# A planner that orders a hybrid decoder step: DVE and POOL take their shared port in turn, and three kinds of matmul get other prices

## The chip, the core and the metric

The kernel runs on one core of a Trainium2 chip. The metric is the device time of one execution in microseconds (us). Engines are named as in the profile: PE is the matrix engine (PEld its weight loads), DVE the vector engine, ACT the scalar engine, POOL the GpSimd engine, SP the queue that issues nearly all DMAs.

## The reference, cut to what matters

One layer on 1024 prompt tokens and 32 sample tokens of width 1024, in float32:

```python
h   = rms_norm(x, norm_mix_w) * (1 + scale_m) + shift_m     # scale, shift, gate from c @ w_ada
p   = h @ w_in
y_a = rwkv7_mixer(...)        # 6 heads of 64, delta rule
y_b = gated_deltanet_mixer(...)   # 6 heads of 64, chunks of 64 tokens
y_c = hgrn2_mixer(...)        # 4 heads of 64, chunks of 64 tokens
x   = x + gate_m * (concat(y_a, y_b, y_c) @ w_out)
h2  = rms_norm(x, norm_ffn_w) * (1 + scale_f) + shift_f
gate, up = split(h2 @ w_ffn_in)
x   = x + gate_f * ((silu(gate) * up) @ w_ffn_out)
y   = rms_norm(x, final_norm_w)
```

The states of the mixers are outputs too. A mixer goes through the chunks one after the other: in a B mixer (`gated_delta_chunked`) each chunk needs the state S that the chunk before it left.

## The kernel before, in words

The kernel is not written in the order in which it runs. Its functions only record operations on a `Plan` object (class `Plan`). Then `nc.order()` (line 2053) decides the order of the whole program, and `emit` (line 619) issues the operations in that order; each engine runs its own in order. About 12,300 matmuls, 4,000 DVE, 2,400 ACT, 1,100 POOL operations and 990 DMAs of SP are recorded. All are issued from line 626 in `emit`, so every row of the profile has the line L626, and tiles tell the rows apart.

`cost` (line 399) gives each operation a price, `hold`, the time for which it keeps its engine, and `LAT` and `SEEN` the time until others see its result. `order` (line 467) walks through a time of its own. At each step it takes the engine that is free first, moves to it the operations whose inputs are there by that time, and issues the one with the lowest key (line 479: the place in the recording, plus a priority). So prices never change what is computed; they change which operations count as ready when an engine comes free, and thereby the order. Two further rules matter on PE. The dense products (float32r, 256 and more moving columns, below written as dense matmuls) of the projections carry a priority that puts them behind everything else, so they fill the time in which the mixers' small matmuls are not ready. And a rule that counts the columns issued lately puts dense matmuls first where the array's clock would fall.

The work, in the order of the recording:

1. Norm and projections (`dense`, line 1501). A float32 product is done as three float32r passes over halves: `wh` times the high part, `wh` times the low part, `wl` times the high part (`dmm`, line 1493). `wh` is rounded by ACT, `wl` is the difference, taken by POOL or DVE (`wtile`, line 1461).
2. Eight mixers (three A, three B, two C) in three segments each; the projections of one run beside the mixer before. `seg_b` (line 1175) has the chunk loop of mixer B: matmul with S, `zs` on DVE, matmul, `us` on ACT, `sd` on POOL, matmul, new S on DVE. Pairs of 64x64 matmuls on the two halves of the rows are issued together (`mm2`, line 721). A triangular inverse per segment is a chain of small DVE operations on the tiles `itq` and `ix`.
3. Output projection, then the feed-forward part, in two halves g = 0 and g = 1 of 528 columns. For each of 22 blocks of 128 rows, `ffn_up` (line 1729) makes seven block products of 12 dense matmuls with 264 columns; their weight sums (tiles `wr`, `int`, `s`, `tq`) and splits (`wl`) go to POOL or DVE by the string `ENGW` (line 70). After each two blocks `down` (line 2018) adds 16 products to the residual with DVE (`gated_half`, line 1789: tiles `kp`); in g = 1 the sample columns need two more DVE operations each (`gated_seq`, line 1798: `ga`, then `kp<-kp,ga`).
4. The final norm.

All four engines' placements (which engine does what) are fixed in the recording.

Of the kernel before, what the change touches and what calls it, by code (L numbers as in the profile page):

```python
# [21 lines left out]
P = 128  # L22
TP = 1024
NQ = 8
TQ = 4
TS = NQ * TQ
T = TP + TS
# [142 lines left out]
ENG = {"tensor": mybir.EngineType.PE, "vector": mybir.EngineType.DVE, "scalar": mybir.EngineType.Activation,  # L170
       "gpsimd": mybir.EngineType.Pool, "sync": mybir.EngineType.SP}
LAT = {"tensor": 158, "vector": 92, "scalar": 110, "gpsimd": 45, "sync": 900}       # result visible after the engine
SEEN = {"tensor": 100, "vector": 36, "scalar": 38, "gpsimd": 64, "sync": 60}        # wait for another engine
# [6 lines left out]
class Tile:  # L180
    def __init__(self, plan, tag, dt):
        self.plan, self.tag, self.dt = plan, tag, dt
        self.slot = self.fresh = self.ap = None
        self.first = None          # first op
        self.left = 0
        self.ops = []
        self.end = 0
        self.writes, self.reads = [], []


class View:
    """a view of a tile whose place is not decided yet; kept as the view of the first place and the way to it"""
# [37 lines left out]
class Op:  # L230
    __slots__ = ("i", "eng", "fn", "args", "kw", "pre", "succ", "npre", "hold", "lat", "ready", "prio", "cols", "wait", "dense", "new", "tiles",
                 "label", "end", "start", "after", "x", "next", "load")
# [10 lines left out]
class Plan:  # L243
    """stands for nc and the tile pools while a program is written down"""
# [15 lines left out]
    # ---- tiles  # L260
    def tile(self, pool, shape, dt, tag, bufs=1, like=None):
        """like: a view of the same shape; such a tag takes both float32 and float32r"""
# [3 lines left out]
        t = Tile(self, tag, dt)  # L266
# [5 lines left out]
    def give(self, tag, to, cut):  # L272
        """once the last tile of tag is done with, the parts that cut makes of its places hold tiles of the tag to"""
        for ap in self.phys[tag]:
            for part in cut(ap):
                self.gifts.setdefault(tag, []).append((to, len(self.phys[to])))
                self.phys[to].append(part)
# [10 lines left out]
    # ---- what a view covers  # L288
    def cover(self, v):
# [6 lines left out]
        else:  # L296
            ps = ap.ap[0][0]
# [4 lines left out]
        if m is None:  # L302
            m = 1
            for s, n in dims:
# [4 lines left out]
                while k < n:  # L309
                    c = min(k, n - k)  # L310
                    # add c more copies
# [6 lines left out]
    # ---- writing down  # L318
# [29 lines left out]
    def glue(self, ops):  # L348
        """to be issued one right after the other, once all of them can be"""
# [14 lines left out]
    def dep(self, o, p, kind):  # L364
        # kind 2: result needed, 1: only the order matters
# [32 lines left out]
    # ---- prices  # L398
    def cost(self, o):
# [7 lines left out]
        e = o.eng  # L407
        if e == "tensor":
# [11 lines left out]
            # hold: how long the next one has to wait; load: how long after the one before the weights are there  # L420
# [5 lines left out]
            elif r:  # L426
                o.hold = max(M, n) / 2.4 + 3 if n >= 256 else max(M / 1.2, n / .6)
            elif K <= 32 and M <= 32:
                o.hold = 56 if p0 == 32 else 27
            elif K <= 64 and M <= 64:  # L430
                o.hold = 27 if p0 >= 64 else 2 * max(M, n) / 1.2 + 3
# [34 lines left out]
    # ---- the order  # L466
    def order(self):
# [12 lines left out]
        # queue of the tiles of each tag  # L480
# [16 lines left out]
        bw = [0.0]  # L497
        warm = {}
# [15 lines left out]
        def grant(tag):  # L514
            q, f = queue[tag], free[tag]
            while f and head[tag] < len(q):
                # earliest free place
# [15 lines left out]
        while len(seq) < n:  # L533
# [39 lines left out]
            if e == "tensor":  # L573
                if last:
                    tm = max(tm, last.start + o.load * (2 if last.x > last.hold else 1))
                last = o
            o.start = tm
# [65 lines left out]
class Step:  # L643
# [7 lines left out]
    # tiles of one tag are given out in program order, so every stream of work has its own  # L651
# [73 lines left out]
    def tokens(self, arrs, c, nch):  # L725
        """chunk c of each array [(h, d), tokens] -> psum [64 tokens, array, h, d]; two chunks are turned at once"""
# [8 lines left out]
    def headsum(self, x, n, which="bones", alloc=None):  # L735
        """sum or mean over the channels of a head, on each of its channels; the ones are exact in float32r"""
# [8 lines left out]
    def sigmoid(self, out, x, nbias=0.0, sign=1.0):  # L745
        """sigmoid(sign * x - nbias) from the one table set that has exp and ln"""
# [12 lines left out]
    def table(self, name, behind=None, before=None):  # L759
        """load a set of functions, behind one activation and before another"""  # L760
# [7 lines left out]
    # tt[(h,s), c, t] holds N^T, N = -(strictly lower part); on return it holds ((I - N)^-1)^T  # L768
    def invert(self, tt, nc_):
# [11 lines left out]
        # one 32x32 block and every fourth column of it per partition:  # L781
        # nt[p, j, i] = N[i, j]; x[p, m, i] = X[i, 4m + cg], X = (I - N)^-1
# [26 lines left out]
        # (T21)^T = (N21 T1)^T T2^T  # L809
# [24 lines left out]
    def raw_a(self):  # L834
        """three segments of [last column of the one before | columns]; the last one ends in 8 x (prev, 4 samples)"""
# [19 lines left out]
    def shift_mix(self, out, r, mu, si):  # L855
        """out = p + mu * (prev - p)"""
# [26 lines left out]
    def mixer_a(self, g, rps, st0, outs):  # L883
        """rps: raw segments of r, k, v; st0 dram [128 (h,dk), 8, 64]; outs: prompt state, sample states, y"""
# [9 lines left out]
    def seg_a(self, g, si, rps, Ss, st0, outs):  # L894
# [70 lines left out]
        for c in range(nch):  # L965
# [13 lines left out]
            # one bank per chunk: z, u, new state, output; a group starts on the operand that comes last  # L979
# [51 lines left out]
    def sample_state(self, xs, st0):  # L1031
        """rows of x^T S0_q of each sequence's own tokens, 32 per x and head"""
# [46 lines left out]
    def raw_b(self, cst):  # L1079
        """three segments of [3 columns before | columns]; the last one ends in 8 x (3 before, 4 samples)"""  # L1080
# [28 lines left out]
    def evac_gates(self, gd):  # L1109
        """rows 0-5 beta_pre, rows 32-37 a_pre of one segment (rounded weights; the rest of the weights 64 rows on)  # L1110
        -> beta, g, exp(g_last - g) of the tokens [(h, token), which, pair, chunk], and beta, g as rows in dram"""
# [7 lines left out]
        def f(si, ps):  # L1119
# [12 lines left out]
            # g = -exp(A_log) * softplus(a + dt_bias)  # L1132
# [11 lines left out]
            # exp(g_last - g)  # L1144
# [30 lines left out]
    def seg_b(self, g, si, rps, z, Ss, st0, outs):  # L1175
# [76 lines left out]
        # the rows of (I - N)^-1 times beta: what it multiplies is v - k S  # L1252
# [58 lines left out]
    def evac_plain(self, z, pad=None):  # L1311
        """the projection as it is; the padding of the last segment"""
# [15 lines left out]
    def lower_bound(self):  # L1328
        nc = self.nc
        # softmax over the depth axis (one layer), then cumsum minus the first layer's share  # L1330
# [16 lines left out]
    def seg_c(self, j, si, q, pf, v, z, Ss, st0, outs):  # L1347
# [39 lines left out]
        def fill(out, mask, data, last, lm):  # L1387
            """the places of A that the mask names; last: of the chunk of the sequences"""
# [4 lines left out]
        # a token with itself and with the one in front of it: products summed over the channels  # L1393
# [67 lines left out]
    def wtile(self, w, eng=None):  # L1461
        """w: dram [128, n, 128] -> for each of the n tiles hi (rounded to the float32r grid), lo = w - hi (exact)"""
# [15 lines left out]
    def wtile_narrow(self, w):  # L1478
        """w: 64 columns, twice: hi of the first half of the columns, lo of the second"""
# [13 lines left out]
    def dmm(self, o, terms, first=True, last=True):  # L1493
        """o = sum of w^T x over terms ((w hi, w lo), (x hi, x lo))"""
# [6 lines left out]
    def dense(self, w, xs, chunks, evac, banks=None, wt=None, warm=0):  # L1501
        """banks: one for each chunk; the products then go through the rows of w first"""
        nc = self.nc
        with self.nc.priority(-LOW):
            wt = wt or self.wtile(w)
            term = lambda k, a, b: (wt[k], (xs[k][0][:, a:b], xs[k][1][:, a:b]))
            if banks:
                pss = [bk() for bk in banks]
                # the array's clock rises with work: products that nothing reads, while the first
                # operands are still on their way  # L1510
# [664 lines left out]
```

## Time and profile before

| what | value |
|---|---|
| three runs | 1862.27, 1865.06, 1881.21 us, median 1865.06 us |
| profiled execution, first to last instruction (span) | 1864.7 us |
| PE busy | 1715.9 us, 92% of the span |
| DVE busy | 1557.1 us, 84% |
| ACT busy, POOL busy | 952.0 us (51%), 958.8 us (51%) |
| TensorE clock granted, mean over the span | 0.953 of full speed |

The profile gives the span of the profiled execution and no other time of it; the span lies 0.4 us below the median of the three runs. Busy time of PE holds modelled ends of pipelined matmuls. A DVE operation that waits for something within its execution counts as busy there.

### The profile page before, as it was taken

Reading aid. Unit: us, or ns where it says so; the run is one execution under the profiler, and the core shown is the slowest. Engines: PE = TensorE matmul, PEld = TensorE weight load, DVE = VectorE, ACT = ScalarE, POOL = GpSimd, SP = SyncE. Lnnn points to the kernel's source line nnn. Section 1 sums busy time; section 2 is a strip of 40 time slices with the busy share of each in tenths; the row PEclk is TensorE's granted clock in tenths of the full one; section 3 lists DMA queues with packets and bytes.
Section 4 is the critical chain, followed back from the end, with each engine's and each line's share of the span. In section 5 each row is a group of like instructions: output and inputs, shape, how many; then the busy total and the mean of one; then the engine's idle time right before and its main releaser. Section 6 shows DMA issues by size and latency. Waiting matters only on the chain.

```text
span 1864.7 us, 42417 instructions
## 1 busy us (share of the span) xinstructions
PE 1715.9 (92%) x15462; PEld 1483.8 (80%) x15462; DVE 1557.1 (84%) x3981; ACT 952.0 (51%) x2383; POOL 958.8 (51%) x1089
## 2 busy tenths in 40 slices
PE   4999999899899789899999999999998889999996
PEld 2777766667677677677679999999998789999995
DVE  6776688879879877887776999889999999899998
ACT  4543454655556455656874655444444543443444
POOL 5542333433335544636523866656567555555555
PEclk8989999889999898999989999999999799999998
DMA  7424123123224222211353222323232132232231
GB/s 264 124 64 116 39 62 109 49 68 113 59 77 127 55 63 55 57 34 39 102 155 115 66 93 95 108 91 109 91 103 69 62 115 79 91 108 85 87 108 65
DMA packets 151242, 166.56 MB, mean 89 GB/s; under 512 B 65941, under 2 KB 91161, under 8 KB 151033
## 3 DMA queue, kind: packets, MB, share of 16 engines
q1 hardware_dynamic: 150456, 163.27, 28.8%
q8 instruction: 121, 1.98, 0.5%
q14 instruction: 89, 0.72, 0.1%
q10 hardware_dynamic: 576, 0.59, 0.1%
HBM read 149.23 MB, written 14.57 MB: 88 GB/s over the span
## 4 chain that ended last, share of the span: by engine, by line
PE 52%; DVE 28%; issue 6%; POOL 5%; ACT 4%; SPq 2%; DMA 2%; DVEq 0%; POOLq 0%; ACTq 0%
PE psd L626 16%; PE psc L626 13%; PE psm L626 11%; PE psg L626 11%; DVE sl L626 6%; DVE itq L626 5%; DVE ix L626 5%; DVE kp L626 3%; SPq L626 2%; POOL wl L626 2%; DVE s L626 2%; ACT sl L626 2%; DVE wl L626 2%; DVE wr L626 2%; DVE act L626 1%
## 5 line engine op out<-in xcount | busy, mean ns | idle before, releaser
L626 PE MATMUL psd<-act,wh 128*128 128x384 f32 (+3 forms) x2144 | 552.8, 334 | 13.2 <-ACT act L626 7.4
L626 PEld LDWEIGHTS psd<-act,wh 128*128 128x128 f32 x2144 | 373.9, 195 | 40.8 <-ACT act L626 8.9
L626 POOL TENSOR_TENSOR wl<-wr,wh 128x512 fp32r<-128x512 f32 (+1 forms) x216 | 300.7, 1396 | 192.1 <-ACT wh L626 177.3
L626 PE MATMUL psd<-act,wl 128*128 128x384 f32 (+3 forms) x1048 | 348.9, 333 | 5.3 <-DVE wl L626 3.8
L626 ACT ACTIVATE sl<-sl 128x384 f32<-128x384 f32 (+5 forms) x400 | 188.1, 484 | 129.2 <-DVE sl L626 101.4
L626 ACT CAST wh<-wr 128x512 fp32r<-128x512 f32 (+1 forms) x280 | 170.7, 615 | 109.0 <-PE psd L626 27.8
L626 PEld LDWEIGHTS psd<-act,wl 128*128 128x128 f32 x1048 | 203.7, 194 | 21.2 <-DVE wl L626 6.2
L626 DVE TENSOR_TENSOR itq<-int,ix 96x66 f32<-96x66 f32 (+26 forms) x558 | 170.7, 306 | 27.1 <-DMA int<-mb 15.9
L626 DVE TENSOR_TENSOR ix<-ix,itq 96x66 f32<-96x66 f32 (+26 forms) x558 | 164.7, 295 | 9.6
L626 PE MATMUL psg<-act,wh 128*128 128x264 f32 (+2 forms) x784 | 154.2, 290 | 5.3 <-DVE act L626 4.0
L626 PE MATMUL psc<-act,wh 128*128 128x264 f32 (+2 forms) x776 | 152.4, 289 | 0.8 <-DVE act L626 0.6
L626 PE MATMUL psm<-act,wh 128*128 128x264 f32 (+1 forms) x760 | 147.8, 288 | 2.7 <-ACT act L626 1.3
L626 POOL TENSOR_TENSOR sl<-sl,sl 128x384 fp32r<-128x384 f32 (+5 forms) x84 | 85.5, 1019 | 101.2 <-ACT sl L626 39.2
L626 PEld LDWEIGHTS psg<-act,wh 128*128 128x128 f32 x784 | 124.6, 191 | 7.5 <-DVE act L626 4.9
L626 ACT CAST raw<-sl 128x264 fp32r<-128x264 f32 x88 | 36.3, 413 | 173.7 <-DVE sl L626 92.5
L626 PEld LDWEIGHTS psc<-act,wh 128*128 128x128 f32 x776 | 123.1, 190 | 2.4 <-DVE act L626 1.1
L626 PEld LDWEIGHTS psm<-act,wh 128*128 128x128 f32 x760 | 119.5, 190 | 4.5 <-ACT act L626 1.5
L626 POOL TENSOR_TENSOR wl<-int,wh 128x512 fp32r<-128x512 f32 (+1 forms) x63 | 87.9, 1398 | 61.1 <-ACT wh L626 61.0
L626 PE MATMUL psc<-act,wl 128*128 128x264 f32 (+2 forms) x388 | 113.4, 292 | 5.4 <-DVE wl L626 3.7
L626 PE MATMUL psg<-act,wl 128*128 128x264 f32 (+2 forms) x392 | 114.0, 291 | 2.6 <-DVE wl L626 2.1
L626 PE MATMUL psm<-act,wl 128*128 128x264 f32 (+1 forms) x380 | 110.2, 290 | 4.4 <-DVE wl L626 3.0
L626 ACT COPY ts<-psg 64x128 f32<-64x128 f32 (+1 forms) x272 | 75.9, 279 | 69.1 <-PE psc L626 46.1
(324 smaller groups left out, 4481.3 us busy)
## 6 DMA issues: line engine op xcount, KB each, us to landing
wr<-in_w_fi_dram SPq DMA_DIRECT2D x87, 256.0 KB
wr<-in_w_ada_dram SPq DMA_DIRECT2D x80, 256.0 KB
wr<-in_w_in_dram SPq DMA_DIRECT2D x62, 256.0 KB
wr<-in_w_fo_dram SPq DMA_DIRECT2D x51, 256.0 KB
int<-in_w_fi_dram SPq DMA_DIRECT2D x46, 256.0 KB
kp<-in_xT_dram SPq DMA_DIRECT2D x32, 192.0 KB
tq<-in_w_fi_dram SPq DMA_DIRECT2D x23, 256.0 KB
s<-in_w_fi_dram SPq DMA_DIRECT2D x20, 256.0 KB
```

Source lines behind the costliest of these rows:

```text
L626: getattr(getattr(nc, o.eng), o.fn)(*[real(a) for a in o.args], **{k: real(a) for k, a in o.kw.items()})
```

## The change

Four edits; everything else that differs in the file is comments, and line numbers (line 626 of before is line 634 of after).

1. Each operation gets a mark `port`. It is set for a POOL operation with an SBUF input of more than one element per partition, for a DVE operation with two such inputs, and for a DVE `tensor_scalar` or `tensor_copy` with one.
2. In `order`, a marked operation starts no earlier than the end of the marked operation before it, on whichever of the two engines that was. The operation has been chosen by then, so its engine waits with it.
3. A float32r matmul with n >= 256 columns is priced n/2.4 + 12 instead of n/2.4 + 3 ns (264 columns: 122 instead of 113; 384 columns: 172 instead of 163).
4. A 64x64 float32 matmul is priced 58 ns in either half of the rows, instead of 110 in the upper and 27 in the lower half.

```diff
@@ cost
         e = o.eng
+        sb = [a for a in list(o.args[1:]) + list(o.kw.values()) if isinstance(a, View) and self.space[a.t.tag] == "sb" and size(a) > 1]
+
+        o.port = e == "gpsimd" and len(sb) > 0 or e == "vector" and (
+            len(sb) > 1 or len(sb) == 1 and o.fn in ("tensor_scalar", "tensor_copy"))
         if e == "tensor":
...
             elif r:
-                o.hold = max(M, n) / 2.4 + 3 if n >= 256 else max(M / 1.2, n / .6)
+                o.hold = max(M, n) / 2.4 + 12 if n >= 256 else max(M / 1.2, n / .6)
             elif K <= 32 and M <= 32:
                 o.hold = 56 if p0 == 32 else 27
             elif K <= 64 and M <= 64:
-                o.hold = 27 if p0 >= 64 else 2 * max(M, n) / 1.2 + 3
+                o.hold = 2 * max(M, n) / 2.4 + 5
@@ order
         bw = [0.0]
+        port = 0
...
+            if o.port:
+                tm = max(tm, port)
+                port = tm + o.hold
             o.start = tm
```

The order of all engines changes from the first products on. Three places follow, each before and after.

PE in the last B mixer, at the chunk loop of `seg_b` (`zs`, `sd`, `us` and `S` are its steps, `psd<-act` are dense matmuls of a projection). Before:

```order
L626 MATMUL psd_151<-act_123,wh_100 128x384
L626 MATMUL psc_117<-zs_185,kp_68 64x64 x2
L626 MATMUL psd_151<-act_124,wh_100 128x384
L626 MATMUL psd_151<-act_123,wl_105 128x384
L626 MATMUL psd_151<-act_125,wh_100 128x384
L626 MATMUL psd_151<-act_126,wh_100 128x384
L626 MATMUL psd_151<-act_125,wl_105 128x384
L626 MATMUL psd_151<-act_127,wh_102 128x384
L626 MATMUL psc_117<-sd_190,ts_184 64x64 x2
L626 MATMUL psd_151<-act_128,wh_102 128x384
```

The same place after:

```order
L634 MATMUL psc_117<-S_176,kp_86 64x64 x2
L634 MATMUL psg_153<-msk_63,kp_80 128x128
L634 MATMUL psg_153<-msk_63,kp_78 128x128
L634 MATMUL psc_117<-zs_185,kp_68 64x64 x2
L634 MATMUL psc_117<-sd_189,ts_184 64x64 x2
L634 MATMUL psc_117<-kp_84,us_187 64x64 x2
L634 MATMUL psc_117<-kp_69,S_176 64x64 x2
L634 MATMUL psc_118<-S_177,kp_86 64x64 x2
```

The dense matmuls that stood between the steps of the chunk are gone from here; they now stand earlier, in longer rows of their own.

PE in the second half of the feed-forward part, at the first use of a `wl` that DVE makes (`wl_105`, used by `psd_151`). Before:

```order
L626 MATMUL psm_112<-act_121,wl_104 128x264
L626 MATMUL psd_151<-act_123,wh_100 128x264
L626 MATMUL psd_151<-act_124,wh_100 128x264
L626 MATMUL psd_151<-act_123,wl_105 128x264
```

The same place after:

```order
L634 MATMUL psd_151<-act_123,wh_100 128x264
L634 MATMUL psd_151<-act_124,wh_100 128x264
L634 MATMUL psc_118<-act_127,wh_102 128x264
L634 MATMUL psc_118<-act_128,wh_102 128x264
L634 MATMUL psc_118<-act_127,wl_107 128x264
L634 MATMUL psc_118<-act_127,wh_102 128x264
L634 MATMUL psc_118<-act_128,wh_102 128x264
L634 MATMUL psc_118<-act_127,wl_107 128x264
L634 MATMUL psc_118<-act_127,wh_102 128x264
L634 MATMUL psd_151<-act_123,wl_105 128x264
```

Seven matmuls of another product have moved in between the two that need only `wh` and the one that needs `wl`.

DVE at the same block, from the end of the residual additions (`kp`, `ga`) to that `wl_105`. Before:

```order
L626 SCALAR_TENSOR_TENSOR kp_87<-psd_150,mod_89,kp_87 128x232
L626 TENSOR_TENSOR ga_213<-psd_150,mod_89 128x32
L626 TENSOR_TENSOR wl_105<-int_113,wh_100 128x512
L626 TENSOR_TENSOR kp_87<-kp_87,ga_213 128x32
L626 TENSOR_TENSOR sl_1039_38269<-sl_1038_38244,psc_117 128x264
L626 TENSOR_TENSOR wl_107<-wr_99,wh_102 128x512
```

The same place after:

```order
L634 SCALAR_TENSOR_TENSOR kp_87<-psd_150,mod_89,kp_87 128x232
L634 TENSOR_TENSOR ga_213<-psd_150,mod_89 128x32
L634 TENSOR_TENSOR wr_97<-tq_202,int_113 128x512
L634 TENSOR_TENSOR kp_87<-kp_87,ga_213 128x32
L634 TENSOR_TENSOR sl_1039_38253<-sl_1038_38228,psc_117 128x264
L634 TENSOR_TENSOR wl_107<-wr_97,wh_102 128x512
L634 TENSOR_TENSOR wr_96<-wr_97,wr_96 128x512
L634 TENSOR_TENSOR wl_105<-tq_202,wh_100 128x512
```

The weight sums `wr` of this block, which DVE did between the residual additions before, now come behind them, and `wl_107` comes ahead of `wl_105`.

## Rows read from the trace of the kernel before

**Rows 1.** The profile's first part: busy us (share of span), instructions.

```profile
PE 1715.9 (92%) x15462; PEld 1483.8 (80%) x15462; DVE 1557.1 (84%) x3981; ACT 952.0 (51%) x2383; POOL 958.8 (51%) x1089
```

**Rows 2.** Busy us by stretch: length, PE, PEld, DVE, ACT, POOL, PEclk, DMA share, GB/s.

```profile
100.00:910.00 810.00, 744.04 (x7775) 567.56 (x7775) 638.97 (x2016) 441.07 (x1260) 345.77 (x548) 0.94 0.25 69
...
1050.00:1435.00 385.00, 379.91 (x3068) 375.02 (x3067) 351.39 (x691) 182.83 (x376) 240.60 (x182) 1.00 0.30 95
1435.00:1500.00 65.00, 49.34 (x269) 42.33 (x270) 62.18 (x110) 37.27 (x84) 43.26 (x40) 0.74 0.21 66
1500.00:1840.00 340.00, 325.03 (x2588) 318.65 (x2588) 313.34 (x742) 142.17 (x281) 189.31 (x137) 0.99 0.28 90
```

**Rows 3.** Chain that ended last, shares by line: 100 to 910, then 1500 to 1840.

```profile
by line: PE psd L626 18.7%; PE psc L626 11.5%; DVE itq L626 10.8%; DVE ix L626 10.7%; PE psm L626 7.1%; DVE sl L626 7.1%; PE psg L626 6.4%; SPq L626 5.1%; issue 3.7%; ACT sl L626 3.2%; DVE kp L626 2.8%; DMA int<-mb 1.8%; DVE s L626 1.4%; DV
...
by line: PE psg L626 14.9%; PE psm L626 14.9%; PE psc L626 14.3%; issue 13.5%; PE psd L626 13.1%; POOL wl L626 7.8%; DVE wl L626 4.2%; DVE wr L626 4.1%; DVE kp L626 3.3%; DVE sl L626 2.8%; DVE int L626 1.4%; POOL wr L626 1.4%; DVE tq L626 1
```

**Rows 4.** PE's longest waits, 100 to 910: us in total, times, longest us.

```profile
PE psm L626 <- DVE sl L626: 12.9, 10, 3.1
PE psc L626 <- DVE S L626: 9.2, 9, 2.0
```

**Rows 5.** Timeline of PE in mixer A: start us, us, what [idle before].

```profile
193.04 0.33 PE L626 MATMUL psd<-act,wl 128*128 128x384 f32 x1
193.21 0.34 PE L626 MATMUL psd<-act,wh 128*128 128x384 f32 x1
193.48 0.56 PE L626 MATMUL psg<-kp,kp 64*64 64x64 f32 x12
193.98 0.44 PE L626 MATMUL psd<-act,wh 128*128 128x384 f32 x1
194.25 0.34 PE L626 MATMUL psd<-act,wl 128*128 128x384 f32 x1
```

**Rows 6.** Timeline of four engines, one chunk of mixer B.

```profile
693.11 0.33 PE L626 MATMUL psc<-zs,kp 64*64 64x64 f32 x4
...
693.53 0.21 ACT L626 COPY us<-psc 128x64 f32<-128x64 f32 x1 [0.19 <-issue]
...
693.82 0.29 POOL L626 TENSOR_TENSOR sd<-us,tok 128x64 f32<-128x64 f32 x1 [3.72 <-ACT us L626]
...
694.62 0.33 PE L626 MATMUL psc<-sd,ts 64*64 64x64 f32 x4
...
695.09 0.28 DVE L626 SCALAR_TENSOR_TENSOR S<-S,dl,psc 128x64 f32<-128x64 f32 x1 [0.69 <-PE psc L626]
...
697.80 0.33 PE L626 MATMUL psc<-zs,kp 64*64 64x64 f32 x4 [0.56 <-DVE zs L626]
```

**Rows 7.** Timeline of PE in the second half of the feed-forward part.

```profile
1654.94 0.40 PE L626 MATMUL psd<-act,wh 128*128 128x264 f32 x2
1656.00 0.39 PE L626 MATMUL psd<-act,wl 128*128 128x264 f32 x1 [0.65 <-DVE wl L626]
1656.22 0.40 PE L626 MATMUL psd<-act,wh 128*128 128x264 f32 x2
1656.46 0.29 PE L626 MATMUL psd<-act,wl 128*128 128x264 f32 x1
```

**Rows 8.** Timeline of DVE in the same stretch.

```profile
1653.07 1.28 DVE L626 TENSOR_TENSOR kp<-kp,ga 128x32 f32<-128x32 f32 x1
...
1655.87 0.18 DVE L626 TENSOR_TENSOR kp<-kp,ga 128x32 f32<-128x32 f32 x1
...
1663.89 0.42 DVE L626 TENSOR_TENSOR sl<-sl,psm 128x264 f32<-128x264 f32 x1
```

**Rows 9.** Timeline of POOL in the same stretch.

```profile
1652.83 1.47 POOL L626 TENSOR_TENSOR wl<-tq,wh 128x512 fp32r<-128x512 f32 x1 [0.57 <-ACT wh L626]
...
1663.73 1.40 POOL L626 TENSOR_TENSOR wl<-wr,wh 128x512 fp32r<-128x512 f32 x1 [1.33 <-ACT wh L626]
```

**Rows 10.** PE's longest wait from 1500 to 1840.

```profile
PE psc L626 <- DVE wl L626: 3.3, 5, 0.7
```

More of the change, by code (lines that the diff above doesn't have):

```diff
@@ L231 @@
     __slots__ = ("i", "eng", "fn", "args", "kw", "pre", "succ", "npre", "hold", "lat", "ready", "prio", "cols", "wait", "dense", "new", "tiles",
-                 "label", "end", "start", "after", "x", "next", "load")
+                 "label", "end", "start", "after", "x", "next", "load", "port")
 class Engine:
```

## The prediction

> **What bounds the kernel now.** I read the profile's first part, then the busy times by stretch, the chain of waits for two of the stretches, PE's waits, and last the timeline at single places. The reader is to see first that PE is busy for 1715.9 of 1864.7 us and DVE for 1557.1 [rows 1]: two engines near their limit, with 149 us of idle PE to be had. The table by stretch [rows 2] says where. In the first half of the feed-forward part (1050 to 1435) PE idles 385.0 - 379.9 = 5.1 us: it is the bound. In the second half (1500 to 1840) it idles 340.0 - 325.0 = 15.0 us, beside a DVE that is busy 313.3 of 340. At the change of halves (1435 to 1500) PE idles 15.7 us at a granted clock of 0.74, with DVE busy 62.2 of 65. In the mixers (100 to 910) it idles 810.0 - 744.0 = 66.0 us at a clock of 0.94. What is left of the 149 lies in the first 100 us, around the output projection and in the last 25 us.
>
> The chain [rows 3] tells the two kinds of stretch apart. In the mixers PE's four banks have 18.7 + 11.5 + 7.1 + 6.4 = 43.7% of it, DVE's inverse alone (`itq`, `ix`) 21.5%: the path passes to and fro between engines. From 1500 on PE's banks have 57.2%, and POOL's and DVE's weight tiles most of the rest.
>
> **The port is real.** The DVE operation `kp<-kp,ga` with 32 elements took 1.28 us from 1653.07 to 1654.35, and 0.18 us at 1655.87 [rows 8]. POOL's `wl` ran from 1652.83 to 1654.30 [rows 9]: DVE waited to its end. At 1663.89 `sl<-sl,psm`, with one input in PSUM, took 0.42 us though POOL's `wl` ran from 1663.73 to 1665.13 [rows 8, 9]. So edits 1 and 2 mark the right operations, and the old planner placed matmuls behind DVE results that come up to a microsecond later than it thought.
>
> **Edits 3 and 4.** Two dense matmuls of 264 columns start 1656.46 - 1656.22 = 0.24 us apart [rows 7], 0.12 each as now priced (before: 0.113); with 384 columns 193.21 - 193.04 = 0.17 [rows 5], as now priced. Six 64x64 matmuls take 193.98 - 193.48 = 0.50 us up to the next dense one [rows 5], 0.083 each with what the switch costs in it; the new price of 58 ns, the old mean of (110 + 27)/2 = 68 ns. The planner's time comes nearer to the chip's on all three. On the chip no operation gets faster by that; only the order counts.
>
> In a sentence apart: the Trainium skill, page "TensorE: Matmul & The Clock Gate", section "Back-to-back issue gap", gives some 131 ns for a sustained matmul of 512 columns, by which edit 3 would go the wrong way and PE would be planned too slow. The trace disagrees, with 0.17 us for 384 columns [rows 5].
>
> **Term A, fewer switches in the mixers.** A group of small matmuls between dense ones costs PE more than its own time. The dense matmul ahead of it starts 0.27 us before the group instead of 0.17 (193.21 to 193.48), and the first one behind it takes 0.27 again (193.98 to 194.25): 0.20 us. Of the 0.50 us inside, six times 58 ns are 0.35, so 0.15 more may belong to it: 0.20 to 0.35 us for each group [rows 5]. Counted over the whole order of PE, other work breaks into the dense matmuls 507 times before and 406 times now: 101 groups less, which is 20 to 35 us of PE's time. The first order excerpt shows how. Where the path is not on PE this lies beside other work; at PE's 43.7% of the chain [rows 3] the lower end is 0.44 x 20 = 9 us, the upper one 35. I take 22, the middle, as PE is busy 92% of these 810 us.
>
> **Term B, waits in the mixers.** PE's longest waits there are for `sl` and `S` of DVE, 12.9 and 9.2 us [rows 4]; they are what a planner makes that sees DVE too early. I let 25 of the 66 us go, with ends of 0 and 50. Against it stand the new bare places of the first excerpt. Counting, in the order, the steps of a chunk with no dense matmul between a matmul, the operation that reads it, and the next matmul: `zs` 25 instead of 16, `sd` 13 instead of 1, uses of `S` 36 instead of 4 (two to a chunk, so 16 chunks). Their length: from the `zs` matmul (693.11) over `us` and `sd` to 693.82 + 0.29 = 694.11 are 1.00 us; from the `sd` matmul (694.62) to the end of S (695.37) 0.75 us [rows 6]. Four passes of 64x64, some 0.25 us, lie within each, so PE idles 0.75 and 0.5 us. With 0.5 for `zs` too: 12 x 0.75 + 16 x 0.5 + 9 x 0.5 = 21.5 us. That is the price if nothing else waits beneath it; the chunk itself gets quicker, since it took 697.80 - 693.11 = 4.69 us with dense matmuls between [rows 6], and the dense work is then done elsewhere. Net I take -4 us, with ends of -50 and +21.
>
> **Term C, the feed-forward part.** Per two blocks (34.3 us) PE waits for weight tiles three times. At 1656.00 it had sat idle for 0.65 us for DVE's `wl` [rows 7]; rows like it sum to 10.5 us over the four banks in that stretch, of which the largest is given [rows 10]. In the new order seven other matmuls, 7 x 0.12 = 0.84 us, stand ahead of the waiting one (second excerpt): enough for the wait as it was. But DVE comes later too: three weight sums now stand between the end of the residual additions and `wl_105`, and `wl_107` ahead of it (third excerpt), and DVE, busy 313.3 of 340, has 26.7 us to give. So of the 15.0 us I take 8 (ends 15 and, with DVE as bound, -5), of the 5.1 us of the first half 3 (0 to 5).
>
> **Term D, change of halves.** DVE is busy 62.2 of 65 us there and its operations are the same; the eight final-norm operations that stood in one row after it are now split by a `raw` that PE waits for. 3 us, ends 0 and 10.
>
> **At nothing.** The clock: (1 - 0.94) x 810 = 49 us of PE's full speed are lost in the mixers [rows 2]; longer rows of dense matmuls speak for more, bare chunks for less; 0, ends 15 both ways. ACT and POOL, busy 51% [rows 1], keep their operations; what hides their moves is their own idle half, and if that cover is gone, a late `wh` or `wl` shows as in term C. SP's DMAs move with the buffers; the share of the DMA engines is 0.25 to 0.30 [rows 2], and a late one would cost what term C's waits cost. The first 100 us and the end keep nearly their order.
>
> **The sum.** -22 - 4 - 8 - 3 - 3 = -40 us from the profiled execution, whose span of 1864.7 us lies 0.4 below the median of the runs, 1865.06. 1865 - 40 = **1825 us**.
>
> **Rivals.** *Much faster:* term B is what counts, and a planner with true prices removes most unplanned waits. For it: the profile's waits are nearly all for DVE. Against it: the order of the inverse's chain and of the recurrences is given by their inputs, whatever the prices. Terms at their ends: -35 - 40 - 10 = -85, 1780 us.
>
> *Nothing:* DVE and its port bind, and what PE saves is spent waiting for DVE. For it: DVE busy 84% [rows 1], 92% from 1500 on. Then terms A and C shrink to 9 and 0: -9 with B at 0, 1856 us. The Trainium skill, page "SBUF — State Buffer", section "Who interferes with whom", holds that whoever starts first has the shared pair for its whole instruction and the other blocks fully; by that rule an order moves the waits and does not shorten them, as no operation changes engine. The trace agrees on the lock (1.28 us beside 0.18, rows 8); what the sum of the waits becomes no row here can show.
>
> *Slower:* the dense matmuls run out before the recurrences do. In the first excerpt a chunk stands without one. If PE's saving in term A lies beside DVE's inverse (9 us), no old wait goes, the 21.5 us of term B are paid in full and the clock's 15 us with them, the mixers lose 28 us; with -6 in the feed-forward part: 1865 + 22 = 1887 us. It decides once the bare steps are over the saving, at some 20 of them.
>
> *The change doesn't do what it says:* the marks only delay the planner's clock; with every engine delayed alike the order would be the same. The excerpts exclude it.
>
> **Chances.** The forecast (1800 to 1846) 0.50, much faster 0.16, nothing (1846 to 1884) 0.21, slower 0.13. A difference of 1%, some 19 us, is about what a measurement of this kernel tells from no change (its three runs span 1862 to 1881). So faster by over 1%: 0.66, within 1%: 0.21, slower: 0.13. The range reaches from the much faster case, 1778, to 1880, just short of the slower one.
>
> **What would show it.** Term A right: fewer groups of small matmuls in PE's timeline, and PE busy less than 744 us in the mixers; wrong: the mixers as long, PE's idle up by what its busy time fell. Term B: the waits for `sl` and `S` fall; waits for `zs`, `us`, `sd` appear with nothing ahead of them. Term C: PE's waits for `wl` from DVE gone, second half 330 us or less; wrong: the same 34.3 us for two blocks, with DVE busy over 95%. The forecast is wrong if the second half and the mixers both keep their length, or if the granted clock in the mixers leaves 0.92 to 0.97.

## The result: 4.5% slower

The changed kernel takes 1939.34 us (median of 5 runs, 1935.77 to 1951.62), the kernel before 1862.27 us in the same comparison (5 runs): a ratio of 1.0446, 95% interval 1.0423 to 1.047. The two medians alone give 1.0414; the recorded ratio compares fast runs alone. The profiled run of after is the slowest of its five, 1951.62 us, so the two traces differ by 85 us (spans of 1949.8 and 1864.7 us), the medians by 77.

First part of the page of after (answers to [rows 1]):

```profile
PE 1762.5 (90%) x15462; PEld 1515.8 (78%) x15462; DVE 1503.9 (77%) x3981; ACT 962.7 (49%) x2389; POOL 952.2 (49%) x1089
```

DVE's busy time fell by 1557.1 - 1503.9 = 53.2 us with the same 3981 operations. The marked ones account for it: their times add up to 1192 us instead of 1242, those of the others to 539 instead of 538, and 496 of them instead of 596 begin with over 0.3 us of a marked POOL operation still to run. So the marks do what they say, though most of these meetings remain. PE's busy time rose by 46.6 us, for the same matmuls. ACT's six more instructions are loads of its tables (17 instead of 11, 21.8 us instead of 14.1); they lie between 83 and 92 us, ahead of the mixers, and e18_most below has four more than before and loses next to nothing.

Where the time came from: I paired the operations of the two traces by their place in the recording. The mixers' last matmul starts at 974 us before and at 1057 after, 83 us later; from there to the end DVE's operations stay 79 to 86 us late (median of every 50 us). So the mixers lose nearly all of it. By the inverse steps at 459 and 596 us of before, 66 and 74 us of lateness are there, but not all of that is lost at that point: PE has done dense matmuls ahead of time. At one small matmul behind the inverses, which starts at 583 us before and at 672 after, 1673 dense matmuls are done in after and 1339 before. Of the 334, 219 have 384 columns and 115 have 288, which start 0.17 and 0.13 us apart in before: some 53 us of work (an estimate). Yet the rest of the mixers gets only 6 us shorter for it (second and fourth row), at a lower clock:

```profile
100.00:583.00 483.00, 449.77 (x4788) 333.34 (x4788) 382.96 (x1241) 248.09 (x721) 175.93 (x285) 0.93 0.29 80
583.00:974.00 391.00, 356.23 (x3655) 279.25 (x3653) 305.65 (x888) 240.01 (x687) 197.02 (x307) 0.94 0.25 69
...
100.00:672.00 572.00, 524.23 (x5280) 401.81 (x5278) 396.08 (x1326) 278.71 (x792) 212.26 (x336) 0.90 0.27 76
672.00:1057.00 385.00, 324.00 (x3246) 246.53 (x3246) 259.00 (x821) 216.37 (x632) 159.94 (x265) 0.83 0.22 62
```

With the 53 us taken from the first part and added to the second, after loses some 36 us in the first and 47 in the second. The stretches of after that hold the work of [rows 2], and both traces over their whole mixers (busy us by stretch; columns as in [rows 2]); before, then after:

```profile
100.00:970.00 870.00, 802.03 (x8411) 609.34 (x8412) 684.67 (x2122) 486.89 (x1404) 372.95 (x592) 0.94 0.27 75
```

```profile
100.00:910.00 810.00, 720.78 (x7062) 552.18 (x7060) 555.81 (x1873) 398.65 (x1129) 309.40 (x488) 0.88 0.24 67
100.00:1056.00 956.00, 847.24 (x8520) 647.97 (x8520) 654.80 (x2146) 495.01 (x1423) 372.20 (x601) 0.87 0.25 70
...
1131.00:1519.00 388.00, 381.25 (x3049) 373.84 (x3048) 351.42 (x693) 182.41 (x376) 243.36 (x183) 1.00 0.29 93
1519.00:1584.00 65.00, 50.60 (x294) 43.88 (x294) 57.19 (x107) 35.81 (x80) 42.44 (x40) 0.76 0.20 66
1584.00:1924.00 340.00, 328.60 (x2571) 318.43 (x2570) 310.12 (x743) 143.36 (x280) 192.50 (x137) 0.99 0.28 90
```

The 86 us between the two mixer rows split into two halves: PE idles 956.00 - 847.24 = 108.8 us instead of 68.0 (+41), and it is busy 45 us longer, as its granted clock fell from 0.94 to 0.87. TensorE ran at the lower of its two levels (1.2 GHz) for 333 us of the whole run instead of 177, in the mixers for 249 instead of 109 (sums of the clock's records). The feed-forward rows, 81 to 84 us later, hold nearly the same busy times.

Which waits? The chain over the mixers, shares by line, before and then after:

```profile
by line: PE psd L626 18.5%; PE psc L626 11.9%; DVE itq L626 10.0%; DVE ix L626 9.9%; PE psm L626 8.0%; PE psg L626 6.7%; DVE sl L626 6.6%; SPq L626 4.8%; issue 3.7%; ACT sl L626 3.3%; DVE kp L626 2.6%; DMA int<-mb 1.7%; POOL sl L626 1.6%; D
```

```profile
by line: PE psd L634 35.4%; PE psc L634 14.6%; PE psm L634 9.7%; PE psg L634 7.5%; ACT sl L634 4.4%; issue 3.8%; SPq L634 3.1%; POOL sl L634 2.6%; DVE itq L634 1.9%; ACT s L634 1.8%; DVE ix L634 1.7%; ACT ts L634 1.6%; DVE sl L634 1.4%; DMA
...
100.92 8.25 PE psd L634 x47
119.57 7.92 PE psd L634 x44
```

The longest piece of dense matmuls in the chain before:

```profile
111.43 3.30 PE psd L626 x14
```

`psd` holds the dense products. Their share doubled, DVE's inverse (`itq`, `ix`) fell from 19.9% to 3.6%: the chain now runs through long rows of dense matmuls, 47 and 44 in one piece. These two lie in the first 30 us of the mixers. PE's waits in the mixers of after, 100 to 980 (compare [rows 4]), and DVE's longest, before and then after (100 to 970 in both; over after's whole mixers, 100 to 1056, the wait at `S` is 93.4 us):

```profile
PE psc L634 <- DVE its L634: 19.6, 12, 3.7
PE psc L634 <- POOL sd L634: 10.2, 11, 2.0
PE psd L634 <- ACT raw L634: 8.9, 13, 1.4
PE psc L634 <- DVE S L634: 7.1, 13, 1.4
PE psg L634 <- ACT sl L634: 6.9, 8, 1.9
PE psm L634 <- ACT sl L634: 6.6, 7, 2.4
...
PE psm L634 <- DVE sl L634: 0.7, 1, 0.7
```

```profile
DVE S L626 <- PE psc L626: 54.8, 54, 3.2
```

```profile
DVE S L634 <- PE psc L634: 86.3, 64, 5.9
DVE s L634 <- ACT s L634: 20.0, 9, 5.8
```

The wait for `sl` of DVE went from 12.9 to 0.7 us, as hoped; in its place stand waits for ACT, which has no marks, and for POOL, and DVE waits longer for PE. Over the whole mixers PE waits 46 us for ACT (before 9), 19 for POOL (before 4) and 42 for DVE (before 53). No engine is the bound of the new mixers: all four are busy for a smaller share of them than before.

### The profile page after: what moved, and what is told of

Same layout as the page of the kernel before. It is cut to its first block, busy times and chain, and to the rows that moved or that the text cites. A ratio compares the mean times of both kernels' runs of the same rounds, so it can differ in the third digit from the quotient of the medians.

```text
span 1949.8 us, 42326 instructions
## 1 busy us (share of the span) xinstructions
PE 1762.5 (90%) x15462; PEld 1515.8 (78%) x15462; DVE 1503.9 (77%) x3981; ACT 962.7 (49%) x2389; POOL 952.2 (49%) x1089
## 4 chain that ended last, share of the span: by engine, by line
PE 67%; DVE 12%; ACT 8%; issue 4%; POOL 3%; DMA 3%; SPq 2%; DVEq 0%; POOLq 0%; ACTq 0%
PE psd L634 26%; PE psc L634 15%; PE psm L634 13%; PE psg L634 12%; DVE sl L634 3%; ACT sl L634 3%; DVE kp L634 2%; SPq L634 2%; ACT wh L634 1%; DVE wl L634 1%; POOL sl L634 1%; DVE act L634 1%; ACT s L634 1%; DVE itq L634 1%; DVE ix L634 1%
## 5 line engine op out<-in xcount | busy, mean ns | idle before, releaser
L634 PEld LDWEIGHTS psd<-act,wh 128*128 128x128 f32 x2144 | 381.4, 199 | 61.4 <-ACT raw L634 18.9
L634 POOL TENSOR_TENSOR wl<-wr,wh 128x512 fp32r<-128x512 f32 (+1 forms) x197 | 274.8, 1402 | 237.8 <-ACT wh L634 222.3
L634 DVE TENSOR_TENSOR itq<-int,ix 96x66 f32<-96x66 f32 (+26 forms) x558 | 150.4, 269 | 31.4 <-DMA kp<-tb 10.7
L634 POOL TENSOR_TENSOR wl<-int,wh 128x512 fp32r<-128x512 f32 (+1 forms) x81 | 116.2, 1435 | 118.0 <-ACT wh L634 109.0
L634 PE MATMUL psc<-act,wh 128*128 128x264 f32 (+2 forms) x776 | 157.8, 293 | 5.9 <-ACT act L634 3.7
L634 PE MATMUL psg<-act,wh 128*128 128x264 f32 (+2 forms) x784 | 159.0, 292 | 1.8 <-ACT sl L634 0.9
L634 DVE TENSOR_TENSOR ix<-ix,itq 96x66 f32<-96x66 f32 (+26 forms) x558 | 151.4, 271 | 7.5
L634 ACT CAST wh<-int 128x512 fp32r<-128x512 f32 x109 | 66.7, 618 | 100.8 <-PE psm L634 28.7
```

What stands on the lines that cost most here:

```text
L634: getattr(getattr(nc, o.eng), o.fn)(*[real(a) for a in o.args], **{k: real(a) for k, a in o.kw.items()})
```

## The experiments

All ratios are to the kernel before on the same chip. "Old prices" is before plus edits 1 and 2. The last column adds up all rows of PE's waits over that run's mixers.

| run | edit | us | ratio, 95% interval | PE waits |
|---|---|---|---|---|
| before | | | 1 | 66 |
| after | the change | 1939 | 1.0446, 1.0423 to 1.0470 | 106 |
| e1_port | marks alone | 1971 | 1.0623, 1.0582 to 1.0665 | 101 |
| e2_prices | prices alone | 1868 | 1.0055, 1.0033 to 1.0076 | 66 |
| e6_slowdve | no marks, DVE price x 1.3 | 1948 | 1.0480, 1.0441 to 1.0519 | 87 |
| e7_paced | after, dense matmuls paced | 1992 | 1.0724, 1.0683 to 1.0765 | 152 |
| e8_pe_old | PE's order unmarked, others marked | 2044 | 1.1007, 1.0977 to 1.1037 | 115 |
| e9_pe_new | PE's order marked, others unmarked | 2058 | 1.1086, 1.1057 to 1.1115 | 151 |
| e10_sp_new | SP's order marked | 1952 | 1.0515, 1.0478 to 1.0552 | 103 |
| e12_dvp_new | DVE's and POOL's order marked | 2020 | 1.0870, 1.0844 to 1.0896 | 108 |
| e13_half | marks, half turns | 1855 | 0.9981, 0.9959 to 1.0003 | 59 |
| e14_fastdve | no marks, DVE price x 0.8 | 1907 | 1.0257, 1.0217 to 1.0297 | 87 |
| e15_rule | before, eager clock rule | 1880 | 1.0106, 1.0042 to 1.0171 | 70 |
| e16_norule | after without that rule | 1962 | 1.0551, 1.0503 to 1.0600 | 103 |
| e17_balance | marks, DVE and POOL x 0.77 | 1869 | 1.0081, 1.0053 to 1.0110 | 66 |
| e18_most | marks, turns of 0.75 | 1867 | 1.0048, 1.0029 to 1.0067 | 60 |
| e19_half_all | the change, half turns | 1881 | 1.0139, 1.0109 to 1.0170 | 69 |
| e20_noinv | marks but on the inverses | 1942 | 1.0429, 1.0397 to 1.0461 | 86 |
| e21_invonly | of DVE, only the inverses marked | 1898 | 1.0200, 1.0180 to 1.0220 | 79 |
| e22_bal_all | the change, DVE and POOL x 0.77 | 1868 | 1.0044, 1.0022 to 1.0065 | 70 |

**Which edit.** The letters are the theories of the expectations. F was my slower rival (dense matmuls spent early), S blames the 64x64 price, T any new order, P the turn-taking.

e1_port: the marks alone, so edits 3 and 4 are left out. 

> The marks for the shared port alone, the three matmul prices as before. Theory F (fill spent early: a planner that sees DVE and POOL slower issues the dense matmuls earlier, so that the chunks of the mixers later stand without them and the clock falls) expects the loss of the whole change, 1925 to 1945 us. Rival S (the lower price of the 64x64 matmuls misleads the planner) expects about 1865. Rival T (any change to the planner loses, because the old order was a lucky one) expects 1875 to 1945.

e2_prices: the reverse, no marks. 

> The three prices alone, no marks for the port. F expects 1850 to 1880 us, S 1920 to 1945, T 1875 to 1945.

e6_slowdve, in `cost` on before, the branch of DVE:

```diff
+            o.hold *= 1.3
```

> The kernel before with every DVE price times 1.3, no marks and the old matmul prices. In its order the dense matmuls run ahead about as far as in the changed kernel (1602 instead of 1339 of 2358 issued at one place of the third B segment; changed kernel 1673), with half as many more bare steps. F expects 1895 to 1935 us. A rival P (what hurts is the turn taking of DVE and POOL itself, their new order) expects 1855 to 1875. T expects anything from 1875 up.

e7_paced: after, in which a dense matmul may fill a gap only while no more than 30 dense ones are issued above before's count at that point (the rule for the clock stays free to take one).

```diff
+            held = full and not avail["tensor"] and not forced and small < nsmall and big > pace(small)
...
-                if avail[e] or e == "tensor" and full:
+                if avail[e] or e == "tensor" and full and not held:
```

> The changed kernel, marks and new prices kept, but while the mixers run a dense matmul may only be issued up to a pace: so many for so many small matmuls issued as in the order of the kernel before, and 30 more. F expects most of the loss to be gone, 1850 to 1885 us. P and S expect 1920 to 1945, as marks and prices are all still there. T expects more than 1875.

The marks cause the whole loss, and the prices give a part of it back (1.0623 to 1.0446); alone they cost half a per cent. Paired by place as above, the mixers of e1_port end 85 us late, as those of after do (83), and 28 us more come behind them: what the prices give back lies there. S falls. P's forecast for e6_slowdve fails: a plan without marks that only holds DVE for slower loses 4.8%. But that is not the same loss: its mixers end 42 us late, and the other half comes in the feed-forward part, where after lost some 3 us. T is weakened, as new orders need not cost much (e2_prices half a per cent, e13_half below nothing at all), and not excluded, as no run here is faster than before beyond the noise. Pacing made it worse, against F; but PE then waited 152 us in the mixers, as it was held back with nothing else to do, so the run does not settle F.

**Whose order.** Two plans in one program: the order of some engines comes from the first, that of the others from a second plan that follows it (here e8; the others name other engines, and their first plan is the marked one).

```diff
+    nc.order(False)
+    nc.order(True, {e: [o for o in nc.seq if o.eng == e] for e in ("tensor",)})
```

> Two plans in one program (old prices): PE keeps the order of the plan without marks (the order of before), and DVE, POOL, ACT and SP are ordered by a second plan with the port marks, which follows that PE order. The marks alone took 1971 us. Theory Q (PE's order is what loses: dense matmuls placed ahead of ready chain steps, so that the chain stands in PE's queue): near before, 1855 to 1895 us. Theory D (the order of DVE and POOL, or of ACT and SP, is what loses): 1930 to 1980 us.

> The mirror of it (old prices): PE keeps the order of the plan with marks, and the other four engines are ordered by a second plan without marks. Theory Q: it keeps the loss, 1930 to 1980 us. Theory D: it loses the loss, 1860 to 1900 us.

> Only SP's queue (DMA issues) keeps the order of the plan with marks; PE, DVE, POOL and ACT are ordered by a second plan without marks that has to live with it (old prices). Theory W (the weight loads and the transfers of the inverse stand behind one another in SP's queue, and this passes the loss on): 1930 us or more. Theories Q and D: below 1900 us, as SP's queue is not what they are about.

> Only DVE and POOL keep the order of the plan with marks; PE, ACT and SP are ordered by a second plan without marks (old prices). Theory D: 1930 us or more. Theory Q: part of the way only, as PE's order then comes from a plan that sees no port, 1870 to 1920 us. Theory W: below 1900 us.

All four lose, the mirror pair e8 and e9 both 10%. W's forecast for SP's queue came (1952 us, 5.2%), but as every mixture lost, that told no theory from another: in these four, an engine's order was worth something only with the orders it was planned with.

**Early or late, and the rule for the clock.** e14_fastdve is e6 with 0.8; e13_half has `port = tm + o.hold * .5`. e15_rule makes the rule that puts dense matmuls first eager, e16_norule takes it out (each cut to what differs):

```diff
-("slack", 200)
+("slack", 1000)
```

```diff
-                if not src or must or 0 < run < RUN or full[0] < src[0]:
+                if not src or 0 < run < RUN or full[0] < src[0]:
```

> Before, without marks, with every DVE price times 0.8: the other side of the run with 1.3, which took 1948 us. Theory O (the orders of a planner that takes results of DVE and POOL for early are the good ones here, since a step that stands too early in a queue costs an idle moment, one that stands too late waits for all that is ahead of it): 1845 to 1875 us. Theory T (the order of before is a lucky one and any other price of DVE loses, or the price of before is the best): 1885 us or more.

> The marks alone (old prices), but the port is taken for half of each marked operation only. Theory O: between before and the full marks (1971 us), 1885 to 1930 us. If the loss comes from any turn-taking, however short: 1940 us or more. If it comes only past some point: below 1875 us.

> Before, without marks, with the rule that puts dense matmuls ahead of ready small ones made eager (its margin 1000 instead of 200 columns): it then decides 459 matmuls of the mixers instead of 113, 73 us of them instead of 17; in the changed kernel 256, 75 us. Theory M (this rule is the way by which the marks lose: a planner that sees DVE late fears for the clock and spends dense matmuls ahead of ready steps): 1915 to 1950 us. If the rule is not the way: 1850 to 1885 us.

> The changed kernel (marks and new prices) with that rule off: a dense matmul goes ahead of a ready small one by the key alone. Theory M: most of the loss gone, 1865 to 1900 us. If the rule is not the way, and the clock needs it: 1940 to 2000 us.

The rule is not the way: eager it costs 1.1%, without it after gains nothing. O falls as well: DVE seen too early costs 2.6%, which is what T expected. Half turns cost nothing, below what O said. So the length of the turns matters: whole ones cost 6.2%, half ones nothing.

**The balance.** e17_balance, on the marks with old prices; e22_bal_all is the same edit on the whole change; e18_most has 0.75 for e13's 0.5; e19_half_all is e13 with the new prices.

```diff
+        if e in ("vector", "gpsimd"):
+            o.hold *= .77
```

> The marks at full length (old prices), with every price of DVE and POOL, and so every turn of the port, times 0.77: the turns stay whole, but the two engines are no later in the plan beside PE and ACT than they were in before. Theory B (DVE and POOL late in the plan beside PE and ACT is what loses): 1850 to 1890 us, and DVE's waits for PE in the mixers back to 90 to 120 us. Theory R (turns of full length order badly by themselves): 1930 us or more.

> The marks alone (old prices) with the port taken for 0.75 of each marked operation; 0.5 gave 1855 us, 1 gave 1971 us. Theories B and R: between them, 1880 to 1940 us. If single orders scatter and there is no such course: outside of that.

> The whole change, new prices too, with the port taken for half of each marked operation. Theory B: the prices did next to nothing without marks (ratio 1.0055) and the half turns alone neither (0.9981): 1845 to 1880 us. If the new prices and the marks work on each other: outside of that.

> The whole change, marks and new prices, with every price of DVE and POOL times 0.77. Theory B: 1860 to 1890 us (the marks with 0.77 gave a ratio of 1.0081, the prices 1.0055), against 1939 for the change as it is. If the new prices of PE bring a loss of their own beside the marks: 1900 us or more.

Windows of 100 to 970, e17_balance and then e20_noinv:

```profile
100.00:970.00 870.00, 800.96 (x8422) 609.10 (x8420) 697.81 (x2133) 488.56 (x1414) 381.04 (x590) 0.92 0.26 77
```

```profile
100.00:970.00 870.00, 787.82 (x8104) 606.11 (x8102) 652.09 (x2073) 468.51 (x1351) 367.27 (x578) 0.91 0.25 71
```

DVE's longest wait in e17_balance:

```profile
DVE S L636 <- PE psc L636: 48.5, 45, 3.7
```

With all marks, but the prices of DVE and POOL and with them the turns at 0.77, the loss is gone (1.0081; with the new prices 1.0044 instead of 1.0446). The mixers do as many matmuls in 870 us as before (8422 against 8411), and DVE's wait for PE at `S` is 48.5 us, as before and not 86.3. Its waits for PE in the mixers add up to 88 us, just under the 90 to 120 expected (before: 109, after: 171). But the port is no freer: 640 marked DVE operations begin with over 0.3 us of a marked POOL operation to run, more than the 596 of before. So 0.77 removes the loss and what the marks had won with it.

e18_most came out below its 1880 to 1940, the case that its expectation gave to orders that scatter; the loss is no straight line in the length of the turn, it comes between 0.75 and 1. e17's turns are 0.77 as long as well, so the two runs don't tell shorter turns (R) from lower prices of DVE and POOL (B). What the runs do show is two groups: the four with whole turns at the old prices of DVE and POOL (after, e1, e7, e16) lose 4.5 to 7.2%, the five with shorter ones (e13, e17, e18, e19, e22) at most 1.4%. Scatter alone would hardly part them so. e19_half_all is 1 us above its range; with half turns the new prices cost some 1.6%, while with full ones they gave about as much.

F is not excluded by these runs either. Ahead of the small matmul of the table above, PE's order has 1339 dense matmuls in before, 1673 in after and 1646 in e18_most (counted in the orders). Bare `sd` steps (the second mark of F): 1 before, 13 in after, 11 in e18_most. The two parts of e18_most's mixers:

```profile
100.00:610.00 510.00, 494.19 (x5177) 377.15 (x5178) 399.10 (x1312) 274.63 (x780) 207.31 (x320) 0.94 0.29 83
610.00:978.00 368.00, 320.85 (x3270) 243.87 (x3271) 267.90 (x824) 218.76 (x640) 167.62 (x271) 0.86 0.23 66
```

Its second part is 23 us shorter than before's for 307 dense matmuls fewer, some 49 us of work by the same count, and has a clock of 0.86: some 26 us are lost there as well, as F describes it. e18_most comes out even because its first part takes only 27 us longer for the 49, with PE idle for 15.8 us; after's takes 89 us longer for the 53, with PE idle for 47.8.

**Which operations.** The inverses' steps are 1,116 of the 1,693 marked DVE operations that run from 100 to 970 us in before.

```diff
+        if e == "vector" and isinstance(out, View) and out.t.tag in ("itq", "ix"):
+            o.port = False
```

> All marks at full length (old prices) but for the steps of the triangular inverses on DVE (tiles itq and ix), which neither wait for the port nor take it in the plan. If the inverses planned late behind POOL are the way (theory I): 1855 to 1890 us, against 1971 with all marks. If the rest of the marks does it: 1930 us or more.

> The mirror: POOL's marks, and of DVE's those of the inverses' steps alone (old prices). Theory I: 1920 us or more. If the rest of the marks does it: below 1885 us. If both this and its mirror are near before, the loss needs all the lateness together, as theory B has it with no one culprit.

Without the inverses' marks 4.3% remain, with them alone 2.0%; both together 6.2%. No one group is the culprit, and e20_noinv's mixers do 8104 matmuls in the 870 us instead of 8411 (second row above). In the mixers the two parts are near each other: they end 41 us late without the inverses' marks and 35 with them alone, 85 with all; the other 31 us of e20_noinv come behind the mixers, by the pairing of its trace.

## Why the prediction was wrong, step by step

- **The port**: right. In before some 510 DVE `tensor_tensor` with both inputs in SBUF began with over 0.3 us of a marked POOL operation still to run, 0.78 us in the median, and took 0.59 us longer (median) than with the port free. Some 500 two-input operations with one input in PSUM began beside POOL in the same way and took no longer. After spends less on it: DVE's busy time -53 us.
- **"The planner's time comes nearer to the chip's on all three"**: true, and the step from it to a better order failed. By the planner's own clock the mixers (the DVE and POOL operations that run from 100 to 970 us in before) take 628 us in before and 817 in after, where the chip took 870 and 956. So the plan of after is the nearer one, and its order the worse one. I took an order made with better prices for a better order; the four plans with whole turns at full prices lose 4.5 to 7.2%. My reading is that what counts is how the engines stand to one another in the plan: the marks lengthen DVE's and POOL's time alone, and by the whole rest of a turn (0.78 us where the chip took 0.59), while ACT's prices stayed early (389 us for its operations of the mixers, where the chip was busy for 487). PE's were about right but for the clock: 571 us, beside the 562 estimated under term A. For it: DVE's price alone costs 4.8% (x 1.3) and 2.6% (x 0.8), and 0.77 makes the marks harmless. Against it: e18_most plans its mixers at 750 us and loses nothing, e6_slowdve at 743 and loses 42 us in them. It is argued, not shown.
- **Term A** (-22): the groups became fewer, 507 to 406, and their saving can only be estimated. With every matmul counted at the time from its start to the next one's that its pair of shapes takes (lower quartile in before), PE's work in the mixers is 562 us before and 546 after, 16 us less; with the times of both traces at the higher clock 10 less. So the term was right in kind and nearer to its lower end of 9 us, and what it saved was covered by the waits and the clock. The sign I had named, PE busy less than 744 us from 100 to 910, came (720.78), but because less of the work was done by then, 7062 matmul records instead of 7775.
- **Term B** (-4): mis-sized, with the sign wrong: PE's waits in the mixers rose by 40 us (66 to 106). The price of a bare step was right in the one chunk looked at. The chunk of [rows 6] in after (timeline of PE):

```profile
762.82 0.33 PE L634 MATMUL psc<-zs,kp 64*64 64x64 f32 x4
763.88 0.33 PE L634 MATMUL psc<-sd,ts 64*64 64x64 f32 x4 [0.73 <-POOL sd L634]
764.69 0.33 PE L634 MATMUL psc<-kp,us 64*64 64x64 f32 x4 [0.48 <-DVE S L634]
...
765.58 0.48 PE L634 MATMUL psc<-zs,kp 64*64 64x64 f32 x4 [0.32 <-DVE zs L634]
```

  0.73 and 0.48 us idle, where I had 0.75 and 0.5, and the chunk takes 2.76 instead of 4.69 us. What I missed are the other waits: for `its` (19.6 us), for ACT's `raw` and `sl`, and DVE's for PE.
- **Clock** (0, ends 15): mis-sized. 0.94 became 0.87, 45 us of PE's busy time. The text had said that a clock outside 0.92 to 0.97 makes the forecast wrong, and it did. Whether the gaps or the clock came first in a given stretch the runs don't tell.
- **Term C** (-11): nothing gained. From 1050 us of before on DVE's operations stay 79 to 86 us late; the first half takes 388 us instead of 385, the second 340 as before. PE's wait for DVE's `wl` [rows 10] went, and POOL's took its place (PE's waits, 1584 to 1924):

```profile
PE psm L634 <- POOL wl L634: 3.2, 6, 1.7
PE psg L634 <- POOL wl L634: 1.9, 5, 0.7
PE psd L634 <- POOL wl L634: 1.5, 5, 0.3
PE psc L634 <- POOL wl L634: 1.1, 4, 0.3
```

  7.7 us of them, for 10.5 of DVE's before: the rival "nothing" had the time of this stretch right, though the wait that took over is POOL's. **Term D** (-3): PE busy 50.60 of the 65 us instead of 49.34, no gain in the length.
- **The slower rival** had the side right, and not the price (28 us in the mixers, measured 83). Its mechanism, dense work that runs out, is seen in the second part of the mixers (some 47 us lost there in after), but it doesn't make the loss by itself: e18_most has the early dense work and the bare steps too, wins in the first part what it loses in the second, and takes 1867 us.
- **The range**: the "much faster" case is given as 1780 and as 1778 us; the sum, 1865 - 85, gives 1780.

What stays open: why the loss comes so steeply between turns of 0.75 and 1, that is, what makes the first part of after's mixers so much longer than e18_most's with nearly the same dense work ahead. My reading of the waits is argued, not shown by a run of its own: each engine runs its queue in order, so a step that the plan takes for late is put behind work for which it then has to wait, as behind the 47 dense matmuls of the chain, and the waits of every engine grow. Nor is it excluded that the order of before is a lucky one among many.

## What to carry to other kernels

A plan that comes nearer to the chip's time need not give a better order: here the nearer plan lost 4.5%. Before one engine's waits are priced truly, see whether the others' are, and try the new ones scaled (here 0.77 made 1.0446 into 1.0044, which is no gain on before either). Judge such a change by the waits between engines in the trace, not by how near single prices come; DVE's busy time fell by 53 us here and the kernel lost 77. Fewer switches and shorter chunks were both there in after, and the mixers still took 83 us longer. And when the same operation is late in two traces, count the other work done ahead of it first: lateness is not yet loss.

## What was unexpected of the hardware

The lock works against POOL as well. `wl<-wr,wh` on DVE, 1180 to 1260 of after (ns, min/median/max):

```profile
L634 DVE TENSOR_TENSOR wl<-wr,wh x6: 682/1362/1771, 1201.0 to 1251.9; 128x512 fp32r<-128x512 f32 x6
```

Alone it takes 0.68 us, behind a POOL operation up to 1.77. POOL's 512-element `tensor_tensor` took 1.30 us with the port free and 1.48 us when it began while a marked DVE operation ran, with 0.33 us of that left (medians of before, some 30 and over 200 operations). So on either side the wait is 0.15 to 0.19 us shorter than the rest of the other's turn. The Trainium skill, page "SBUF — State Buffer", section "Who interferes with whom", says that whoever issues first has the shared pair for the whole instruction and the other blocks; the trace agrees on who waits, and shows a part of the wait hidden: DVE waited 0.59 us where 0.78 were left.
